# Rows of the first combine loaded ahead of and between the attention's first weight slabs, with the sums of its norm on ScalarE

## The chip, the cores and the metric

The kernel runs on one core of one Trainium2 chip. A core has a matrix engine (TensorE, PE in the profile), a vector engine (VectorE, DVE), an activation engine (ScalarE, ACT), a general engine (GpSimd, POOL) and a queue engine (SyncE, SP) from which nearly all loads are issued. Each engine runs its own instructions in the order in which they stand and waits for the others by semaphores. The metric is the device time of one execution in microseconds; less is better.

## The reference, cut to what matters

Two layers over 1024 tokens of 1024 numbers. Each has a mixer and a mixture of experts (MoE), and each of these four is followed by a layer norm. The change lies where the first layer ends and the second begins:

```
ffn = _hierarchical_moe(x, ...)                          # layer 0
x   = _layer_norm(DEEPNORM_ALPHA * x + ffn, g, b)        # "the first combine"
qkv = x @ w_qkv                                          # layer 1: dilated attention
...
def _layer_norm(x, g, b):
    mu = mean(x);  var = mean((x - mu)**2)
    return (x - mu) * rsqrt(var + 1e-5) * g + b
```

The attention's product needs normed rows, so nothing of it can start before the first tile of 128 rows has its norm.

## The kernel before, in words

Rows are worked on in eight tiles of 128. During the MoE the sum `ALPHA * x + ffn` (divided by `ALPHA`) gathers in a DRAM tensor `S`: GpSimd scatters the experts' outputs into it with an adding DMA (L1111). After the last scatter stands a loop over overflow blocks, which runs zero times on these inputs; all engines meet at its end (L1273).

Then `attn_phase` begins. Its `stream` walks over "pieces" of w_qkv, 512 columns each; piece 0 makes K of the first half. A piece is loaded as four slabs `wr` of 256 rows (L1418); ScalarE rounds each into `wh` (L176), VectorE takes the rest into `wl` (L177). `Moe.rows` loads a tile of `S` into a buffer `pre` (L1297), `Moe.combine` norms it and stores it to the DRAM tensor `x` (L1303). `prep` transposes a normed tile on TensorE (L1454), eight blocks in two halves, into `tr`, and splits each half into `xh` (ScalarE) and `xl` (VectorE). One tile of a piece is then 8 steps of three products, `wh*xh`, `wl*xh`, `wh*xl` (L181 to L183), and its result is taken out as `qk`.

`layer_norm` takes mean and variance on VectorE (two BN_STATS, L190; one BN_AGGR, L192), adds the epsilon (L193), raises to -1/2 on GpSimd (L194), and then makes two passes on VectorE: `(a - mean) * g` (L196) and `a * rstd + b` (L197). The last norm of the kernel, `Moe.finish`, takes its sums on ScalarE instead: a Copy with scale -1/D that accumulates the negative mean (L1316) and a Square that accumulates the variance (L1317).

A scheduler puts the instructions of each engine into one order from the order of the code and its own clock; what it made of the two kernels is shown with the change.

Of the kernel before, what the change touches and what calls it, by code (L numbers as in the profile page):

```python
# [11 lines left out]
F32 = mybir.dt.float32  # L12
# [3 lines left out]
AF = mybir.ActivationFunctionType  # L16
ALU = mybir.AluOpType
# [4 lines left out]
P = 128  # L22
D = 1024
T = 1024
NT = T // P
# [34 lines left out]
BETW = 1  # L60
LATE = (0, 0)
XACT = (0, 1)
EXTRA = 4
HB = 3
CUT = 1
# [14 lines left out]
def dap(ap, off, dims):  # L80
    return bass.AP(tensor=ap.tensor, offset=ap.offset + off, ap=[list(d) for d in dims])
# [104 lines left out]
def layer_norm(nc, cm, pool, dst, src, g, b, last=False, eng=None):  # L186

    st = pool.tile([P, 2, 6], F32, name="ln_st", bufs=2)
    for i in range(2):
        nc.vector.bn_stats(st[:, i, :], src[:, i * 512:(i + 1) * 512])  # L190
    mv = pool.tile([P, 4], F32, name="ln_mv", bufs=2)
    nc.vector.bn_aggr(mv[:, 0:2], st.rearrange("p a b -> p (a b)"))  # L192
    nc.vector.tensor_scalar(mv[:, 2:3], mv[:, 1:2], EPS / ALPHA2, None, op0=ALU.add)  # L193
    nc.gpsimd.tensor_tensor(mv[:, 3:4], mv[:, 2:3], cm.mhalf, op=ALU.pow)  # L194
    if last:
        nc.vector.scalar_tensor_tensor(src, src, mv[:, 0:1], g, op0=ALU.subtract, op1=ALU.mult)  # L196
        nc.vector.scalar_tensor_tensor(dst, src, mv[:, 3:4], b, op0=ALU.mult, op1=ALU.add)  # L197
        return
    nc.vector.scalar_tensor_tensor(mv[:, 2:3], mv[:, 0:1], -1.0, mv[:, 3:4], op0=ALU.mult, op1=ALU.mult)
    nc.scalar.activation(src, src, AF.Identity, scale=mv[:, 3:4], bias=mv[:, 2:3])  # L200
    (eng or nc.vector).tensor_tensor(src, src, g, op=ALU.mult)
    nc.gpsimd.tensor_tensor(dst, src, b, op=ALU.add)
# [735 lines left out]
class Moe:  # L938
# [6 lines left out]
    def run(self, extra=lambda tmp: None):  # L945
# [273 lines left out]
        for n in range(N + 1):  # L1219
            st = steps[n] if n < N else None  # L1220
            before = steps[n - 1] if n else None
            if n == PLAN:
                plan = rt.plan(sp, sp.tile([P, 512], F32, name="h", bufs=2), lambda s: ps.tile(s, F32, name="tr"))
                tab, base = plan[2:]
                more(plan)
            if n == STEPS.index("D") - PLD:
                tok, gate = place(slice(OV, OV + 1), kp.tile([P, 2048], F32, name="pre3"), "tok1")
                d = steps[STEPS.index("D")].blocks[1]
                d.tok, d.gate = tok[:MORE], gate[:MORE]
            if n == 0:  # L1230
                steps[0].x = [rows_in(steps[0], blocks[0])]
            if st:
                gathers(blocks.index(st.blocks[-1]) + 5 if n >= PLAN else FIXED)

            def between():
                if n > 1:
                    rows_out(steps[n - 2])
                if n:
                    before.h = [sides(before, h, "h" + "d" * i) for i, h in enumerate(before.h)]

            if st:
                if n >= FIXED:
                    st.U, st.W = parts(*(of_expert(nc.sync.value_load(tab[0:1, OV + 1 + r:OV + 2 + r], min_val=0, max_val=31))
                                         for r in st.experts))
                if n:
                    load(st.U)
                pg = up(st, between)
            with behind(tc, *first, *self.loads[-1:][:n > 3]):
                if n == 6:
                    t = kp.tile([P, 2048], F32, name="pre4")  # L1250
                    self.lng, self.lnb = t[:, 0:D], t[:, D:]
                    nc.sync.dma_start(self.lng, dap(self.ln_g, 0, [[0, P], [1, D]]))
                    nc.sync.dma_start(self.lnb, dap(self.ln_b, 0, [[0, P], [1, D]]))
                if n == EXTRA:
                    extra(kp.tile([P, D], F32, name="pre2"))
            if n:
                load(before.W)
                if not st:
                    between()
                ws = split_down(before)  # L1260
            if st:
                h = [hidden(b, p, "d" * i) for i, (b, p) in enumerate(zip(st.blocks, pg))]
            if n + 1 < N:
                steps[n + 1].x = [rows_in(steps[n + 1], b, "d" * i) for i, b in enumerate(steps[n + 1].blocks)]
            if n:
                before.p = down(before, ws)
            if st:
                st.h = [hidden_in(x) for x in h]
# [28 lines left out]
        self.tc.nc.sync.dma_start(a, token_rows(self.S, self.rt.runs[i], D))  # L1297
        return a

    def combine(self, i, store):  # L1300
        a = self.rows(i)
        layer_norm(self.tc.nc, self.cm, self.kp, a, a, self.lng, self.lnb, True)
        self.tc.nc.sync.dma_start(token_rows(store, self.rt.runs[i], D), a)  # L1303
        return a

    def finish(self, store):
        nc = self.tc.nc
        rows = [self.rows(i) for i in range(NT)]

        nc.vector.tensor_scalar(self.lng, self.lng, D ** 0.5, None, op0=ALU.mult)  # L1310
        mean, ss = (self.kp.tile([P, NT], F32, name=n) for n in ("f_mean", "f_ss"))
        with self.tc.tile_pool(name="f", bufs=2, reuse_waits="tile") as fp:
            for i in range(NT + 1):
                if i < NT:
                    a, m, s = rows[i], mean[:, i:i + 1], ss[:, i:i + 1]
                    nc.scalar.activation(fp.tile([P, D], F32, name="f_j"), a, AF.Copy, scale=-1 / D, accum_out=m)  # L1316
                    nc.scalar.activation(fp.tile([P, D], F32, name="f_j"), a, AF.Square, bias=m, accum_out=s)  # L1317
                    nc.vector.tensor_scalar(s, s, D * EPS / ALPHA2, None, op0=ALU.add)  # L1318
                    nc.gpsimd.tensor_tensor(s, s, self.cm.mhalf, op=ALU.pow)  # L1319
                    nc.vector.scalar_tensor_tensor(a, a, m, self.lng, op0=ALU.add, op1=ALU.mult)  # L1320
                if i:
                    a, s = rows[i - 1], ss[:, i - 1:i]
                    nc.vector.scalar_tensor_tensor(a, a, s, self.lnb, op0=ALU.mult, op1=ALU.add)  # L1323
                    nc.sync.dma_start(token_rows(store, self.rt.runs[i - 1], D), a)


TWO_PI = 2 * math.pi
# [57 lines left out]
def attn_phase(tc, cm, rope_, xd, before, w_qkv, w_o, ln_g, ln_b, runs, emit):  # L1385
# [6 lines left out]
    with ctx:  # L1392
# [79 lines left out]
        def flip(dst, n, r, tag):  # L1472
# [4 lines left out]
            V.tensor_copy(dst[:, 2 * n:2 * n + a, :], pt)  # L1477
            asked.add(tag)

        def stream():  # L1480

            pieces = [(i, s, 0, 512) for i in range(5) for s in (1, 0, 2)] + [(5, 2, 0, 512)]
# [7 lines left out]
                k -= len(pieces)  # L1490
                return Weights(w_o, 0, 512, slice(k * 512, k * 512 + 512))

            nxt = piece(0).make()
            for c in range(4):
                prep(0, c, before.combine(c, xd))
            pend = []
            for k, (i, s, n, w) in enumerate(pieces):
                g, h = steps[i]
                ws = nxt.make()
                nxt = piece(k + 1).make(1)  # L1500
                if i == 5:
                    yield lambda: 3 in done_att
                for c in range(4):
                    j = 4 * h + c
                    xh, xl = XS[g, j]
                    pq = pmm([P, w])
                    for kk in range(KD):
                        if kk == 4 and w == 512:
                            yield 2700, 0
                        mm3(nc, pq, xh[:, kk, :], xl[:, kk, :], *ws.row(kk), kk == 0, kk == KD - 1)  # L1510
                    if k == 0:
                        before.combine(4 + c, xd)
                        if c == 3:
                            open_late()
                    if s == 2:
                        VT[g, j] = sp.tile([P, 512], F32, name="vt", bufs=8)
                        nc.scalar.activation(VT[g, j], pq, AF.Copy)
                    else:
                        dst = KT if s == 1 else QT
                        if n == 0:  # L1520
                            dst[g, j] = sp.tile([P, 4, P], F32, name="kt" if s == 1 else "qt", bufs=8 if s == 1 else 5)
                        pend.append((dst[g, j], n, rope(g, j, pq), (i, c, n) if s == 0 else None))
                    while len(pend) > (LAG if i < 5 and s != 2 else LAG5 if i == 5 and k + 1 < len(pieces) else 0):
                        flip(*pend.pop(0))
                    if s == 2 and i < 5:
                        g2, h2 = steps[i + 1]
                        for cc in {1: (0,), 2: (1,), 3: (2, 3)}.get(c, ()):
                            prep(g2, 4 * h2 + cc)
                    yield 2700, 0
                if s == 2 and i < 5:  # L1530
                    done_gemm.add(i)
# [291 lines left out]
```

## Time and profile before

| | |
|---|---|
| runs | 2817.41, 2819.85, 2819.84 us; median 2819.84 |
| profiled execution | 2819.68 us, span 2817.9 us |
| busy share | PE 93%, DVE 60%, ACT 44%, POOL 22% |
| mean granted TensorE clock | 0.958 |
| last product of layer 0's MoE | starts at 1463.54 us |
| first transposition of the attention | starts at 1490.76 us |

All places are in us from the start of the span. The hole in TensorE's work between the last two lines is where the change lies; it is about a hundredth of the span.

### The profile page before, as it was taken

Reading aid. Unit: us, or ns where it says so; the run is one execution under the profiler, and the core shown is the slowest. Engines: PE = TensorE matmul, PEld = TensorE weight load, DVE = VectorE, ACT = ScalarE, POOL = GpSimd, SP = SyncE. Lnnn points to the kernel's source line nnn. Section 1 sums busy time; section 2 is a strip of 40 time slices with the busy share of each in tenths; the row PEclk is TensorE's granted clock in tenths of the full one; section 3 lists DMA queues with packets and bytes.
Section 4 is the critical chain, followed back from the end, with each engine's and each line's share of the span. In section 5 each row is a group of like instructions: output and inputs, shape, how many; then the busy total and the mean of one; then the engine's idle time right before and its main releaser. Section 6 shows DMA issues by size and latency. Waiting matters only on the chain. (4 is left out here: it accounts for less than half of the span.)

```text
span 2817.9 us, 40424 instructions
## 1 busy us (share of the span) xinstructions
PE 2609.4 (93%) x14744; PEld 1919.6 (68%) x14744; DVE 1701.0 (60%) x3287; ACT 1250.8 (44%) x1974; POOL 617.5 (22%) x554
## 2 busy tenths in 40 slices
PE   8999999999997999999967999999998899999893
PEld 6778888788874656555636887778886465565562
DVE  5586676897674545645637544555668354466464
ACT  3354443545421544644632444444532254456464
POOL 0054332444351311212111000111112121121112
PEclk9999999999997999999988999999998899999997
DMA  5454543735466899999965432333325899999995
GB/s 147 130 150 135 145 125 105 218 114 155 128 226 223 297 399 378 368 393 373 386 233 213 124 117 73 106 109 107 98 93 195 288 356 387 367 389 388 380 387 190
DMA packets 316415, 647.68 MB, mean 230 GB/s; under 512 B 34172, under 2 KB 202548, under 8 KB 283444
## 3 DMA queue, kind: packets, MB, share of 16 engines
q1 hardware_dynamic: 296660, 594.63, 59.0%
q0 software_dynamic: 14944, 33.64, 5.1%
q10 hardware_dynamic: 4608, 16.78, 1.5%
q8 instruction: 119, 1.95, 0.3%
q14 instruction: 84, 0.69, 0.1%
HBM read 598.15 MB, written 66.19 MB: 236 GB/s over the span
## 5 line engine op out<-in xcount | busy, mean ns | idle before, releaser
L990 DVE TENSOR_TENSOR wl<-wr,wh 128x2048 fp32r<-128x2048 f32 x209 | 477.6, 2291 | 291.9 <-ACT wh L986 227.8
L986 ACT ACTIVATE wh<-wr 128x2048 fp32r<-128x2048 f32 x212 | 405.0, 1916 | 266.0 <-DMA wr<-in_moe_w_down_dram 137.2
L177 DVE TENSOR_TENSOR wl<-wr,wh 128x1024 fp32r<-128x1024 f32 x184 | 239.0, 1300 | 142.2 <-ACT wh L176 137.2
L176 ACT ACTIVATE wh<-wr 128x1024 fp32r<-128x1024 f32 x184 | 194.2, 1055 | 240.5 <-PE mm L182 93.2
L181 PE MATMUL mm<-xth,wh 128*128 128x512 f32 x640 | 255.7, 400 | 1.2 <-DVE carry L391 1.2
L183 PE MATMUL mm<-xth,wl 128*128 128x512 f32 x640 | 254.9, 399 | 0.5 <-DVE wl L177 0.5
L182 PE MATMUL mm<-xtl,wh 128*128 128x512 f32 x640 | 253.3, 396 | 1.7 <-DVE xtl L177 1.7
L181 PE MATMUL mm<-wh,xh 128*128 128x512 f32 (+1 forms) x640 | 248.2, 388 | 0.0
L182 PE MATMUL gu<-wl,xh 128*112 128x512 f32 x576 | 230.3, 400 | 18.2 <-DVE wl L990 15.1
L182 PE MATMUL mm<-wl,xh 128*128 128x512 f32 (+1 forms) x640 | 241.8, 378 | 0.0
L183 PE MATMUL mm<-wh,xl 128*128 128x512 f32 (+1 forms) x640 | 239.8, 375 | 0.0
L181 PE MATMUL gu<-wh,xh 128*112 128x512 f32 x576 | 231.9, 403 | 2.1 <-ACT wh L986 2.0
L183 PE MATMUL gu<-wh,xl 128*112 128x512 f32 x576 | 230.6, 400 | 0.0
L1050 PE MATMUL gu<-wr,xh 128*64 128x512 f32 (+1 forms) x784 | 213.0, 604 | 12.0 <-DMA wr<-in_moe_w_up_dram 11.9
L995 POOL DMA_INDIRECT G<-X,pl_toks x44 | 68.2, 1551 | 557.0 <-PE tr L1011 478.1
L1111 POOL DMA_INDIRECT S<-y,pl_toks x56 | 110.2, 1968 | 327.9 <-ACT y L1109 249.8
L1050 PEld LDWEIGHTS gu<-wr,xh 128*64 128x64 f32 (+1 forms) x784 | 70.3, 145 | 139.3 <-issue 111.3
L182 PEld LDWEIGHTS gu<-wl,xh 128*112 128x112 f32 x576 | 102.0, 177 | 58.3 <-DVE wl L990 21.8
L183 PEld LDWEIGHTS mm<-xth,wl 128*128 128x128 f32 x640 | 121.5, 190 | 27.9 <-issue 1.4
L181 PEld LDWEIGHTS mm<-xth,wh 128*128 128x128 f32 x640 | 121.6, 190 | 27.5 <-issue 1.9
L182 PEld LDWEIGHTS mm<-xtl,wh 128*128 128x128 f32 x640 | 121.4, 190 | 26.7 <-DVE xtl L177 2.0
L182 PE MATMUL dn<-wl,hh 128*112 128x512 f32 x288 | 121.3, 421 | 19.4 <-DVE wl L990 19.4
(485 smaller groups left out, 5404.4 us busy)
## 6 DMA issues: line engine op xcount, KB each, us to landing
wr<-in_moe_w_gate_dram SPq DMA_DIRECT2D x126, 1024.0 KB, 20.4
wr<-in_moe_w_down_dram SPq DMA_DIRECT2D x126, 1024.0 KB, 21.9
wr<-in_moe_w_up_dram SPq DMA_DIRECT2D x124, 1024.0 KB, 21.7
wr<-in_ssd_w_in_dram SPq DMA_DIRECT2D x80, 512.0 KB, 4.0
wr<-in_attn_w_qkv_dram SPq DMA_DIRECT2D x72, 512.0 KB, 4.1
E<-csd SPq DMA_DIRECT2D x32, 512.0 KB, 4.3
wr<-in_ssd_w_out_dram SPq DMA_DIRECT2D x32, 512.0 KB, 4.0
xt<-x SPq DMA_DIRECT2D x24, 512.0 KB, 4.0
```

What stands on the lines that cost most here:

```text
L176: return (nc.scalar.activation(hi, src, AF.Copy), (eng or nc.vector).tensor_tensor(lo, src, hi.bitcast(F32), op=ALU.subtract))
L177: (eng or nc.vector).tensor_tensor(lo, src, hi.bitcast(F32), op=ALU.subtract))
L181: nc.tensor.matmul(out, lhsT=sh, rhs=mh, start=first, stop=False)
L182: nc.tensor.matmul(out, lhsT=sh, rhs=ml, start=False, stop=False)
L183: return nc.tensor.matmul(out, lhsT=sl, rhs=mh, start=False, stop=last)
L986: chain("act", lambda: nc.scalar.activation(wh, wr, AF.Copy))
L990: chain("dve", lambda: nc.vector.tensor_tensor(wl, wr, wh.bitcast(F32), op=ALU.subtract), *gate)
L995: return nc.gpsimd.indirect_dma_start(out=g[:r], out_offset=None, in_=rt.X[:, :], in_offset=bass.IndirectOffsetOnAxis(ap=tok, axis=0), bou ...
L1050: i = nc.tensor.matmul(out[c], lhsT=x[k][:, c], rhs=w[z][:, n], start=first, stop=last)
L1111: nc.gpsimd.indirect_dma_start(out=S[:, :], out_offset=bass.IndirectOffsetOnAxis(ap=tok, axis=0), in_=y[:tok.shape[0]], in_offset=None, bo ...
```

## The change

Four things. (1) `Moe.combine` falls into three: `rows` (the load), `norm` and `normed`. The attention now issues the load of row tile 0 first, then one weight slab of piece 0 and one row tile in turn, and the loads of tiles 5 to 7 after them. Before, all four slabs stood first. (2) The norm is that of `finish`: sums by ScalarE for tiles 1 to 7. Tile 0 keeps BN_STATS, with two small instructions in place of one. The junk output of the two ScalarE passes goes to the buffers `xt`, which the attention uses later. (3) The scaling of `g` by the square root of D, which the form with sums needs, moves from `finish` into the MoE (step 16 in the code) and is done in both layers. (4) `finish` calls the same functions and is otherwise as it was.

```diff
+SCALE = 16
...
+                if n == SCALE:
+                    nc.vector.tensor_scalar(self.lng, self.lng, D ** 0.5, None, op0=ALU.mult)
...
-    def combine(self, i, store):
-        a = self.rows(i)
-        layer_norm(self.tc.nc, self.cm, self.kp, a, a, self.lng, self.lnb, True)
-        self.tc.nc.sync.dma_start(token_rows(store, self.rt.runs[i], D), a)
-        return a
+    def norm(self, i, a, junk, last=False):
...
+        if i or last:
+            nc.scalar.activation(junk(), a, AF.Copy, scale=-1 / D, accum_out=m)
+            nc.scalar.activation(junk(), a, AF.Square, bias=m, accum_out=s)
+            nc.vector.tensor_scalar(s, s, D * EPS / ALPHA2, None, op0=ALU.add)
+        else:
...
+            nc.vector.tensor_scalar(s, mv[:, 1:2], float(D), D * EPS / ALPHA2, op0=ALU.mult, op1=ALU.add)
+            nc.vector.tensor_scalar(m, mv[:, 0:1], -1.0, None, op0=ALU.mult)
+        nc.gpsimd.tensor_tensor(s, s, self.cm.mhalf, op=ALU.pow)
+        nc.vector.scalar_tensor_tensor(a, a, m, self.lng, op0=ALU.add, op1=ALU.mult)
...
+    def normed(self, i, a, store):
+        self.tc.nc.vector.scalar_tensor_tensor(a, a, self.ss[:, i:i + 1], self.lnb, op0=ALU.mult, op1=ALU.add)
         self.tc.nc.sync.dma_start(token_rows(store, self.rt.runs[i], D), a)
...
-            nxt = piece(0).make()
+            nxt, rows = piece(0), [before.rows(0)]
             for c in range(4):
-                prep(0, c, before.combine(c, xd))
+                nxt.make(c + 1)
+                rows.append(before.rows(c + 1))
+                combine(c, rows[c])
+                prep(0, c, rows[c])
+            rows += [before.rows(c) for c in range(5, 8)]
...
                     if k == 0:
-                        before.combine(4 + c, xd)
+                        combine(4 + c, rows[4 + c])
```

SP's queue right behind the loop, before. `pre_13170` holds row tiles 0 and 1, `pre_13225` tiles 2 and 3, and so on; `S_237` is `S`, `x_83` is `x`.

```order
L1418 DMA wr<-in_attn_w_qkv_dram 128x2x512 x4
L1297 DMA pre_13170<-S_237 128x1024 x2
L1297 DMA pre_13225<-S_237 128x1024 x2
L1297 DMA pre_13311<-S_237 128x1024 x2
L1297 DMA pre_13408<-S_237 128x1024
L1418 DMA wr<-in_attn_w_qkv_dram 128x2x512
L1297 DMA pre_13408<-S_237 128x1024
L1418 DMA wr<-in_attn_w_qkv_dram 128x2x512 x3
L1303 DMA x_83<-pre_13170 128x1024 x2
```

The same place of the change (`pre_13147` holds row tiles 0 and 1, `pre_13191` tiles 2 and 3).

```order
L1300 DMA pre_13147<-S_237 128x1024
L1431 DMA wr<-in_attn_w_qkv_dram 128x2x512
L1300 DMA pre_13147<-S_237 128x1024
L1431 DMA wr<-in_attn_w_qkv_dram 128x2x512
L1300 DMA pre_13191<-S_237 128x1024
...
L1300 DMA pre_13284<-S_237 128x1024 x2
L1431 DMA wr<-in_attn_w_qkv_dram 128x2x512
L1328 DMA x_83<-pre_13147 128x1024
L1431 DMA wr<-in_attn_w_qkv_dram 128x2x512
L1328 DMA x_83<-pre_13147 128x1024
```

Row tile 0 went from the fifth place to the first. The three further slabs of piece 1, which stood ahead of all stores of normed rows, now stand one behind each of the first stores.

VectorE's queue at the same place, before.

```order
L177 TENSOR_TENSOR wl<-wr,wh 128x1024 x4
L190 BN_STATS ln_st<-pre_13170 128x6 x4
L192 BN_AGGR ln_mv<-ln_st 128x2 x2
L193 TENSOR_SCALAR ln_mv<-ln_mv 128x1
L196 SCALAR_TENSOR_TENSOR pre_13170<-pre_13170,ln_mv,pre_9802 128x1024
L190 BN_STATS ln_st<-pre_13225 128x6
...
L197 SCALAR_TENSOR_TENSOR pre_13170<-pre_13170,ln_mv,pre_9802 128x1024 x2
...
L177 TENSOR_TENSOR xl<-tr,xh 128x512 x2
```

And in the change (`pre_9802` is the tile with `g` and `b`).

```order
L1317 BN_STATS ln_st<-pre_13147 128x6 x2
L1319 BN_AGGR ln_mv<-ln_st 128x2
L1320 TENSOR_SCALAR f_ss<-ln_mv 128x1
L1321 TENSOR_SCALAR f_mean<-ln_mv 128x1
L1323 SCALAR_TENSOR_TENSOR pre_13147<-pre_13147,f_mean,pre_9802 128x1024
L178 TENSOR_TENSOR wl<-wr,wh 128x1024
L1327 SCALAR_TENSOR_TENSOR pre_13147<-pre_13147,f_ss,pre_9802 128x1024
L1313 TENSOR_SCALAR f_ss<-f_ss 128x1
L1323 SCALAR_TENSOR_TENSOR pre_13147<-pre_13147,f_mean,pre_9802 128x1024
L178 TENSOR_TENSOR wl<-wr,wh 128x1024
L1327 SCALAR_TENSOR_TENSOR pre_13147<-pre_13147,f_ss,pre_9802 128x1024
L178 TENSOR_TENSOR xl<-tr,xh 128x512
```

Before, four slab splits and the statistics of two tiles stood ahead of tile 0's norm, and the first `xl` stood behind both passes of tiles 0 and 1, the first passes of tiles 2 and 3 and the statistics of further tiles. Now tile 0's norm has one split in it, and the first `xl` stands behind the norm of tile 1.

## Rows read from the trace of the kernel before

**Rows 1.** Windows: us, busy us of PE, PEld, DVE, ACT, POOL; clock; DMA share; GB/s.

```profile
1475.00:1490.00 15.00, 0.00 (x0) 0.00 (x0) 12.89 (x19) 4.59 (x5) 3.07 (x2) 0.50 1.04 414
1500.00:1510.00 10.00, 10.00 (x39) 7.97 (x39) 10.00 (x16) 2.25 (x4) 2.71 (x2) 0.77 0.31 127
...
1600.00:1700.00 100.00, 100.00 (x771) 80.42 (x771) 49.45 (x164) 44.92 (x104) 0.00 (x0) 1.00 0.35 107
...
2000.00:2100.00 100.00, 100.00 (x783) 87.09 (x779) 64.45 (x257) 44.17 (x131) 16.83 (x14) 1.00 0.25 80
```

**Rows 2.** Waits, 1455 to 1540: us in total, times, longest.

```profile
PE tr L1454 <- DVE pre L197: 26.8, 1, 26.8
...
PE tr L1454 <- DVE xl L177: 5.0, 1, 5.0
```

**Rows 3.** Timeline of SP's queue: start, us from first to last, line, issues.

```profile
1471.73 1.93 SPq L1418 DMA_DIRECT2D wr<-in_attn_w_qkv_dram  x4
1473.70 4.96 SPq L1297 DMA_DIRECT2D pre<-S  x7
...
1482.19 2.81 SPq L1418 DMA_DIRECT2D wr<-in_attn_w_qkv_dram  x3
```

**Rows 4.** Timeline of ScalarE: the first two slabs and the fourth tile's eviction.

```profile
1475.65 1.06 ACT L176 ACTIVATE wh<-wr 128x1024 fp32r<-128x1024 f32 x1 [11.09 <-DMA wr<-in_attn_w_qkv_dram]
...
1477.00 1.06 ACT L176 ACTIVATE wh<-wr 128x1024 fp32r<-128x1024 f32 x1 [0.29 <-DMA wr<-in_attn_w_qkv_dram]
...
1527.01 0.60 ACT L1461 ACTIVATE qk<-mm 128x512 f32<-128x512 f32 x1 [0.37 <-PE mm L183]
```

**Rows 5.** Timeline of VectorE, 1455 to 1500.

```profile
1476.74 5.27 DVE L177 TENSOR_TENSOR wl<-wr,wh 128x1024 fp32r<-128x1024 f32 x4 [17.42 <-ACT wh L176]
1481.93 2.46 DVE L190 BATCH_NORM_STATS2 ln_st<-pre 128x6 f32<-128x512 f32 x4
1484.31 0.33 DVE L192 BATCH_NORM_AGGREGATE ln_mv<-ln_st 128x2 f32<-128x12 f32 x2
...
1484.61 1.28 DVE L196 SCALAR_TENSOR_TENSOR pre<-pre,ln_mv,pre 128x1024 f32<-128x1024 f32 x1
1485.80 0.68 DVE L190 BATCH_NORM_STATS2 ln_st<-pre 128x6 f32<-128x512 f32 x1
...
1498.09 1.27 DVE L177 TENSOR_TENSOR xl<-tr,xh 128x512 fp32r<-128x512 f32 x2
```

**Rows 6.** Timeline of TensorE at the end of its two waits.

```profile
1490.76 1.97 PE L1454 MATMUL tr<-ident,pre 128*128 128x128 f32 x8 [26.83 <-DVE pre L197]
...
1498.82 1.11 PE L1454 MATMUL tr<-ident,pre 128*128 128x128 f32 x4 [5.04 <-DVE xl L177]
```

**Rows 7.** Timeline of SP's queue at the kernel's end.

```profile
2786.09 3.94 SPq L1297 DMA_DIRECT2D pre<-S  x8
```

**Rows 8.** Timeline of ScalarE at the kernel's end.

```profile
2789.94 1.06 ACT L1316 ACTIVATE f_j<-pre 128x1024 f32<-128x1024 f32 x1 [11.79 <-DMA pre<-S]
...
2792.27 1.04 ACT L1316 ACTIVATE f_j<-pre 128x1024 f32<-128x1024 f32 x1
```

**Rows 9.** All eight raisings to -1/2 of the first combine, grouped by line.

```profile
L194 POOL TENSOR_TENSOR ln_mv<-ln_mv,mhalf 128x1 f32<-128x1 f32 x8 | 13.0, 1632 | 37.5 <-DVE ln_mv L193 37.5
```

**Rows 10.** Window of TensorE alone in which its clock rose: busy, clock, DMA, GB/s.

```profile
1504.00:1505.00 1.00, 1.00 (x6) 0.68 0.00 0
```

**Rows 11.** Waits of SP's queue, 2060 to 2770.

```profile
SPq L971 <- DMA S<-xt: 53.2, 1, 53.2
```

**Rows 12.** Windows in layer 1's MoE, columns as in rows 1.

```profile
2400.00:2500.00 100.00, 96.99 (x438) 60.79 (x437) 53.80 (x37) 52.18 (x49) 18.83 (x11) 0.97 0.99 370
```

**Rows 13.** The scaling of g before (layer 1), by its line.

```profile
L1310 DVE TENSOR_SCALAR pre<-pre x1: 687/687/687, 2327.1 to 2327.1; 128x1024 f32<-128x1024 f32 x1
```

**Rows 14.** Timeline of VectorE in layer 0's MoE, near the new scaling's place.

```profile
1006.41 4.50 DVE L990 TENSOR_TENSOR wl<-wr,wh 128x2048 fp32r<-128x2048 f32 x2 [0.39 <-ACT wh L986]
1014.37 2.29 DVE L990 TENSOR_TENSOR wl<-wr,wh 128x2048 fp32r<-128x2048 f32 x1 [3.46 <-PE gu L183]
```

More of the change, by code (lines that the diff above doesn't have):

```diff
@@ L1298, in rows @@
         return a
-    def combine(self, i, store):
-        a = self.rows(i)
-        layer_norm(self.tc.nc, self.cm, self.kp, a, a, self.lng, self.lnb, True)
+    def norm(self, i, a, junk, last=False):
+        nc = self.tc.nc
+        if not i:
+            self.mean, self.ss = (self.kp.tile([P, NT], F32, name=n) for n in ("f_mean", "f_ss"))
+        m, s = self.mean[:, i:i + 1], self.ss[:, i:i + 1]
+        if i or last:
[3 more added lines that the diff above has]
+        else:
+            st = self.kp.tile([P, 2, 6], F32, name="ln_st", bufs=2)
+            for k in range(2):
+                nc.vector.bn_stats(st[:, k, :], a[:, k * 512:(k + 1) * 512])
+            mv = self.kp.tile([P, 4], F32, name="ln_mv", bufs=2)
+            nc.vector.bn_aggr(mv[:, 0:2], st.rearrange("p a b -> p (a b)"))
+            nc.vector.tensor_scalar(s, mv[:, 1:2], float(D), D * EPS / ALPHA2, op0=ALU.mult, op1=ALU.add)
[4 more added lines that the diff above has]
+        self.tc.nc.vector.scalar_tensor_tensor(a, a, self.ss[:, i:i + 1], self.lnb, op0=ALU.mult, op1=ALU.add)
         self.tc.nc.sync.dma_start(token_rows(store, self.rt.runs[i], D), a)
-        return a
     def finish(self, store):
-        nc = self.tc.nc
         rows = [self.rows(i) for i in range(NT)]
-        nc.vector.tensor_scalar(self.lng, self.lng, D ** 0.5, None, op0=ALU.mult)
-        mean, ss = (self.kp.tile([P, NT], F32, name=n) for n in ("f_mean", "f_ss"))
         with self.tc.tile_pool(name="f", bufs=2, reuse_waits="tile") as fp:
@@ L1314, in finish @@
                 if i < NT:
[L1315 to L1320, printed above, removed]
+                    self.norm(i, rows[i], lambda: fp.tile([P, D], F32, name="f_j"), True)
                 if i:
-                    a, s = rows[i - 1], ss[:, i - 1:i]
-                    nc.vector.scalar_tensor_tensor(a, a, s, self.lnb, op0=ALU.mult, op1=ALU.add)
-                    nc.sync.dma_start(token_rows(store, self.rt.runs[i - 1], D), a)
+                    self.normed(i - 1, rows[i - 1], store)
 TWO_PI = 2 * math.pi
@@ L1478, in flip, with combine @@
             asked.add(tag)
+        def combine(i, a):
+            before.norm(i, a, lambda: sp.tile([P, D], F32, name="xt", bufs=4))
+            before.normed(i, a, xd)
         def stream():
```

## The prediction

> **What bounds the kernel now.** I read the windows first, then the waits, then the queues one by one around the place that the windows point to. In the window from 1475 to 1490 TensorE does nothing at all, while VectorE is busy for 12.89 of 15 us; from 1500 on TensorE is busy for the whole of every window shown, and it stays so through the attention (five windows of 100 us between 1600 and 2100, the first and the last in [rows 1]). So the stretch after the loop is bound by VectorE, and all that follows up to about 2100 by TensorE: what lets TensorE start earlier there moves the whole attention. The waits say the same: the first transposition waits 26.8 us for the second pass of the norm, and after three us of work TensorE waits another 5.0 us for the first `xl` [rows 2]. The queues say why. SP issues four slabs from 1471.73, and the rows of `S` only from 1473.70 [rows 3]; the slabs land 1.35 us apart (1475.65, 1477.00, [rows 4]), and VectorE, which keeps its order, splits all four (5.27 us) before it looks at a row, so its first statistics start at 1481.93 [rows 5]. TensorE starts at 1490.76, and works without a gap from 1498.82 [rows 6].
>
> **The change part by part.** The sum is the move of that 1498.82, built up along VectorE's new order.
>
> *Rows first.* Tile 0's load is now the first issue behind the loop, at 1471.73. How soon such a load lands when it stands first is shown at the kernel's end: issued at 2786.09, used at 2789.94, so 3.85 us [rows 7, 8]. Tile 0 is there at 1475.6. Slabs and rows are both 512 KB; at 1.35 us apiece slab 0 lands at 1476.9, tile 1 at 1478.3, slab 1 at 1479.6.
>
> *Tile 0's norm.* Two BN_STATS take half of the 2.46 us of four, 1.23, to 1476.8. The aggregation and two small instructions take what two aggregations and one small one took, 1484.31 to 1484.61, so 0.3, to 1477.1. A pass over a tile keeps VectorE for 1.20 us (1484.61 to 1485.80), to 1478.3. Then stands slab 0's split, a quarter of 5.27 us, so 1.32; its `wh` is ready at 1476.9 + 1.06 = 1478.0, in time; to 1479.6. The raising on GpSimd (mean 1.63, [rows 9]) began at 1477.1 and ends under these two. Second pass, to 1480.8 [all durations from rows 5]. The first transposition can start there, 9.9 us sooner than 1490.76.
>
> *Tile 1's sums on ScalarE.* Copy and Square of one tile take 2792.27 - 2789.94 = 2.33 us [rows 8]. From 1478.3 they end at 1480.6, before VectorE is free: this is work taken off VectorE (1.23 + 0.2 us a tile, seven times) and put on an engine that is busy 4.59 of 15 and 2.25 of 10 us there [rows 1]. ScalarE's added 7 x 2.33 = 16.3 us lie beside VectorE's work as long as no Square ends after VectorE asks for it; I cost them at nothing for tile 1, and take the rest up as a rival.
>
> *The first xl.* From 1480.9: pass 1 of tile 1 to 1482.1, slab 1's split (`wh` at 1480.6 + 1.06 = 1481.7) to 1483.4, pass 2 to 1484.6, `xl` (half of 1.27) to 1485.2. Before, TensorE worked on behind that `xl` from 1498.82. The difference is 13.6 us.
>
> *From there to the end of piece 0.* Before, the four tiles took until 1527.0, when the fourth is taken out [rows 4]: 28.2 us, of which TensorE ran the first 5.8 at half rate, since its clock rises between 1504 and 1505 (mean 0.68 in that window, [rows 10]). With the same 28.2 the new end is 1513.4. The other limit is VectorE. Its work from 1475.6 to the last `xl` of piece 0 is 1.5 (tile 0's statistics) + 16 passes x 1.20 + 5 splits x 1.32 + 8 `xl` x 0.63 + about 2 of small ones and of the rotation of two results, so 34 us, to 1509.8. Half a tile of products follows; 28.2 us with 5.8 at half rate are 25.3 at full rate for four tiles, so half a tile is 3.2, to 1513.0. TensorE's limit is the later by a little, so 13.6 us stand, and more than 14 cannot come out here.
>
> *SP's stores between the slabs of piece 1.* Their loads now stand behind stores that wait for normed tiles (1480.8, 1484.6, and, with the same steps carried on for tiles 2 and 3, 1489.5 and 1495.1). The last slab of piece 1 is so issued by about 1495 and lands by 1499, where it was issued by 1485 [rows 3]. Piece 1 begins at 1513; the cover is 14 us, and this costs nothing. If it were gone, each us of lateness would be one on the path.
>
> *Scaling g in the MoE.* One instruction of 0.69 us [rows 13]. In layer 1 it was already there, since the scheduler had pulled it out of `finish`. In layer 0 it is new and stands between the two splits that start at 1006.41; VectorE waits 3.46 us soon after [rows 14]. I take nothing, and 0.7 as the upper bound.
>
> The sum: 2819.68 - 13.6 = 2806.1 us for the profiled execution, which lies 0.16 under the median of the runs; I say 2806.
>
> **A rule weighed.** TensorE stood still for 26.8 us [rows 2], its clock went to half rate (0.50 in the first window of [rows 1]), and it rose only 5.8 us after the work had become gapless; the three us of work from 1490.76 that a wait ended did not lift it [rows 6, 10]. The Trainium skill ("TensorE: Matmul & The Clock Gate", section "HAM oscillation — how this bites in real kernels") says that the throttled rate is the default and that matmul work in bursts with waits between them keeps falling back to it. By that rule an earlier start with small waits in it gains less than the start moves. The trace agrees so far as it goes. The row alone gives -13.6, the rule the time of the first rival.
>
> **The rivals.**
>
> *The clock stays at half rate through the new stretch.* In the new order TensorE is fed in portions: `xl` of tile 2 stands on VectorE behind two passes and a split, at about 1500 to 1501. If the small waits before it keep the clock at 1.2 GHz until then, instead of 1491, ten us are worked at half rate and five are lost: -8.6, 2811. For it: the burst of [rows 6] that did not lift the clock. Against: behind 1485.2 my steps leave no wait over 1 us.
>
> *ScalarE's sums arrive late.* ScalarE keeps its order, and its Copies wait for rows to land ahead of `xh` evictions that TensorE needs. Sums 16.3, five slabs 5.2, eight `xh` and two `qk` 5.6 us: 27 us in the same 34. Each Square that ends after VectorE asks for it adds to VectorE's limit. Two or three late by 1.5 to 2 us cost 4: 2810. For it: slack of only a few us on either engine. Against: tile 1's sum, the tightest, is in time by 0.3.
>
> *The gain is given back later.* Layer 1's MoE keeps the DMA engines at a share of 0.99 [rows 12]. Were its weight stream to start no sooner, the time would stay 2819.7. Against: the first wait of that stream on SP's queue is one of 53.2 us for a result of the attention [rows 11], which comes sooner with it.
>
> *Slower: SP's queue holds the weights back.* SP issues nothing while it waits for a store. If a normed tile comes late, all slabs behind it are late; piece 1's last slab, wanted some 4 us into the piece, must be issued by about 1513 (3.85 us to land). From there each us costs one; at 1527 the gain is gone, and at 1530 the time is 2823. That needs tile 3's norm to end 35 us behind my 1495, 9 us more for each of the first four. For it: the order on SP. Against: nothing in the trace makes a tile's norm that long.
>
> **How the numbers follow.** Forecast, 2804 to 2808: 0.60. Clock low: 0.12. Late sums: 0.16. Given back: 0.07. Slower: 0.05. The two middle rivals give 2810 to 2812, so the range ends at 2812; below, VectorE's limit (-14) and the runs' own spread of 2.4 us give 2803. A measurement can tell about 0.2%, 5.6 us, from no change, so faster means under 2814.2: 0.60 + 0.12 + 0.16 = 0.88; same 0.08 (given back, with the milder half of slower); slower 0.04.
>
> **What would show it.** In the new profile the first transposition starts near 1481 and the first `wh*xl` product near 1485; the fourth `qk` of piece 0 is taken out near 1513; the windows through the attention stay full; the end of the attention and the span move by the same amount. A first transposition at 1481 with a fourth `qk` later than 1516 makes the feeding steps wrong (the clock row tells which rival); a moved `qk` without a moved span makes the third rival right.

## The result, and the profile after

The change takes 2803.48 us (median of 6 runs, 2799.09 to 2807.32) where the kernel before took 2819.07 beside it (6 runs, 2817.41 to 2823.37): a ratio of 0.9945, 95% interval 0.9935 to 0.9956. That is 15.6 us, by the interval 12 to 18. The profiled execution took 2806.40 us (before 2819.68), so 13.3 less; the forecast was 2806.1. Two executions, one of e3_warm (2979.07 us, mean granted clock 0.817) and one of the change beside e9_filled_again (4532.87 us, 0.715), ran at a lower clock and are left out of every time and comparison here.

Two executions start the stretch of the change at slightly different places (the last product of layer 0's MoE at 1463.54 before, at 1462.56 after). So from here on a place is also given in us behind that product, which is called P. From P to the end of the span it is 1354.4 us before and 1342.1 after: of the 13.3 us, 12.3 lie behind P and 1.0 ahead of it.

The first windows, to be laid beside [rows 1] (columns as there):

```profile
1475.00:1490.00 15.00, 8.64 (x25) 6.57 (x26) 14.45 (x20) 13.96 (x22) 4.75 (x3) 0.50 1.03 399
1490.00:1500.00 10.00, 10.00 (x50) 8.18 (x50) 10.00 (x16) 10.00 (x20) 5.90 (x3) 0.99 1.04 407
1600.00:1700.00 100.00, 100.00 (x764) 80.53 (x762) 48.01 (x160) 46.21 (x108) 0.00 (x0) 1.00 0.33 103
```

TensorE is busy for 8.64 us of a window in which it did nothing, and for all of the next. The price stands in ScalarE's column: from 1475 to 1500 it is busy for 23.96 of 25 us. The attention further on is as it was.

The waits from 1465 to 1540 that answer to [rows 2] (us in total, times, longest):

```profile
PE tr L1467 <- DVE pre L1327: 16.9, 1, 16.9
...
PE tr L1467 <- DVE f_ss L1313: 1.3, 1, 1.3
DVE pre L1327 <- POOL f_ss L1322: 0.5, 1, 0.5
ACT xt L1311 <- DMA pre<-S: 0.2, 1, 0.2
PE mm L182 <- ACT xh L177: 0.2, 1, 0.2
```

26.8 became 16.9, and 5.0 became 1.3. The last three are what the prediction costed at nothing, and together they are under 1 us. The 1.3 is written down to the small instruction behind the first `xl`; what TensorE waited for is that `xl`.

VectorE's new order, for [rows 5]:

```profile
1474.34 1.29 DVE L1317 BATCH_NORM_STATS2 ln_st<-pre 128x6 f32<-128x512 f32 x2 [16.15 <-DMA pre<-S]
...
1478.49 1.28 DVE L1327 SCALAR_TENSOR_TENSOR pre<-pre,f_ss,pre 128x1024 f32<-128x1024 f32 x1
1479.68 0.15 DVE L1313 TENSOR_SCALAR f_ss<-f_ss 128x1 f32<-128x1 f32 x1
...
1482.61 1.28 DVE L1327 SCALAR_TENSOR_TENSOR pre<-pre,f_ss,pre 128x1024 f32<-128x1024 f32 x1 [0.45 <-POOL f_ss L1322]
1483.81 0.68 DVE L178 TENSOR_TENSOR xl<-tr,xh 128x512 fp32r<-128x512 f32 x1
...
1507.26 0.68 DVE L178 TENSOR_TENSOR xl<-tr,xh 128x512 fp32r<-128x512 f32 x1
```

SP had issued tile 0's load at 1470.80; VectorE starts on it 3.54 us later (the forecast took 3.85). The first `xl` ends at 1484.49, and the last of piece 0 at 1507.94. ScalarE, GpSimd and TensorE beside it:

```profile
1478.21 1.15 ACT L1312 ACTIVATE xt<-pre,f_mean 128x1024 f32<-128x1024 f32 x1
1479.27 0.19 ACT L1312 ACTIVATION_READ_ACCUMULATOR xt<-pre,f_mean 128x1 f32 x1
...
1479.92 2.66 POOL L1322 TENSOR_TENSOR f_ss<-f_ss,mhalf 128x1 f32<-128x1 f32 x1 [3.20 <-DVE f_ss L1313]
```

```profile
1479.82 1.97 PE L1467 MATMUL tr<-ident,pre 128*128 128x128 f32 x8 [16.87 <-DVE pre L1327]
...
1484.55 1.12 PE L1467 MATMUL tr<-ident,pre 128*128 128x128 f32 x4 [1.35 <-DVE f_ss L1313]
1485.31 0.78 PE L184 MATMUL mm<-wh,xl 128*128 128x512 f32 x1
...
1489.73 0.63 PE L182 MATMUL mm<-wh,xh 128*128 128x512 f32 x1
1490.15 0.44 PE L183 MATMUL mm<-wl,xh 128*128 128x512 f32 x1
```

Tile 1's sum is there at 1479.46, and VectorE asks for it at 1479.68. The raising of that sum takes GpSimd 2.66 us, and VectorE waits 0.45 us for it. Behind the first `xl` TensorE works without a gap; its products take 0.63 us each until the clock rises at about 1490.2 (0.50 before, 0.99 behind, in the windows above).

In the later rows little else changed. The long wait of layer 1's weight stream is 53.5 us, was 53.2 [rows 11], and the first load behind it is issued at 2111.48 where it was issued at 2125.52, so the stream moved with the attention. The scaling of `g` shows up twice, 0.69 us each, at 1007.8 and 2312.7:

```profile
SPq L972 <- DMA S<-xt: 53.5, 1, 53.5
```

```profile
L1256 DVE TENSOR_SCALAR pre<-pre x2: 687/688/689, 1007.8 to 2312.7; 128x1024 f32<-128x1024 f32 x2
```

### The profile page after: what moved, and what is told of

Its sections match the earlier page's. It is cut to its first block, busy times and chain, and to the rows that moved or that the text cites. A ratio compares the mean times of both kernels' runs of the same rounds, so it can differ in the third digit from the quotient of the medians.

```text
span 2804.7 us, 40430 instructions
## 1 busy us (share of the span) xinstructions
PE 2606.4 (93%) x14744; PEld 1918.7 (68%) x14744; DVE 1690.6 (60%) x3268; ACT 1266.0 (45%) x2002; POOL 618.3 (22%) x554
## 5 line engine op out<-in xcount | busy, mean ns | idle before, releaser
L182 PEld LDWEIGHTS mm<-xth,wh 128*128 128x128 f32 x640 | 121.6, 190 | 28.2 <-issue 1.9
```

Of the source, the lines that this page charges most:

```text
L182: nc.tensor.matmul(out, lhsT=sh, rhs=mh, start=first, stop=False)
```

## The experiments

All places in this table are us behind P, read from the timelines. "First transposition" and "resumes" are the starts of TensorE's `tr` and of its first `wh*xl`; "piece 0" is the end of the last product of piece 0's fourth tile; "last vt" is the start of the last `vt` eviction, near the end of the attention's products; "last y" that of the last expert output of layer 1.

| kernel | first transposition | resumes | piece 0 | last vt | last y |
|---|---|---|---|---|---|
| before | 27.22 | 36.04 | 63.38 | 542.31 | 1314.01 |
| the change | 17.26 | 22.75 | 49.49 | 528.94 | 1301.09 |
| e7_after_again | 17.47 | 22.97 | 49.48 | 528.94 | 1300.55 |
| e9_after_beside | 16.84 | 22.33 | 48.55 | 528.00 | 1298.78 |
| e1_loads_only | 18.03 | 23.47 | 58.26 | 537.20 | 1307.25 |
| e2_sums_only | 23.71 | 29.98 | 57.16 | 536.13 | 1307.90 |
| e4_more_act | 17.07 | 23.17 | 50.07 | 529.03 | 1300.29 |
| e5_all_sums | 17.97 | 23.47 | 49.83 | 529.28 | 1300.98 |
| e3b_warm | 16.83 | 22.11 | 49.02 | 528.46 | 1300.32 |
| e6_warm_pool | 16.99 | 22.39 | 50.63 | 530.07 | 1301.57 |
| e8_warm_filled | 17.31 | 21.91 | 47.27 | 526.46 | 1297.47 |
| e9_filled_again | 16.62 | 21.94 | 47.28 | 526.51 | 1298.70 |

The column "piece 0" does not hold the same work in all rows. A finished tile's `qk` is later transposed on TensorE in a group of four blocks. Two such groups stand ahead of the end of piece 0 in the kernel before (where that end is at 1526.92):

```profile
1520.80 0.60 PE L1476 MATMUL tr<-ident,qk 128*128 128x128 f32 x4
...
1524.01 0.60 PE L1476 MATMUL tr<-ident,qk 128*128 128x128 f32 x4
```

In the change the scheduler put the second one behind it (the end is at 1512.05):

```profile
1506.42 0.60 PE L1489 MATMUL tr<-ident,qk 128*128 128x128 f32 x4
...
1513.48 0.60 PE L1489 MATMUL tr<-ident,qk 128*128 128x128 f32 x4
```

e1, e2 and e4 have two groups in piece 0 like the kernel before, all other rows have one like the change. A group is worth 0.5 us: from piece 0's end to piece 1's it is 23.7 us with four groups and 24.2 with five. So rows with a different number of groups are compared at the last `vt`.

**One part alone.** e1_loads_only keeps the new order of loads and takes the statistics of all tiles on VectorE:

```diff
-        if i or last:
+        if last:
```

> The new load order with BN_STATS for all eight tiles (no sums on ScalarE in the first combine). All anchors are taken from the last product of layer 0's MoE, as differences to the kernel before. Theory: the load order moves the first transposition (about -9), but VectorE keeps 7 x 1.4 = 10 us more work than in the change, and piece 0 becomes VectorE's: end of piece 0 at -4 to -7, time 2813 to 2816. Rival (the load order is the whole gain, the sums on ScalarE only move work off an engine that did not limit): end of piece 0 at -13, time 2805 to 2807.

e2_sums_only keeps ScalarE's sums and puts the loads back into the old order:

```diff
-            nxt, rows = piece(0), [before.rows(0)]
+            nxt, rows = piece(0).make(), []
...
-                nxt.make(c + 1)
-                rows.append(before.rows(c + 1))
+                rows.append(before.rows(c))
...
-            rows += [before.rows(c) for c in range(5, 8)]
...
+                        rows.append(before.rows(4 + c))
```

> The old load order (four slabs first) with the sums of tiles 1 to 7 on ScalarE. Theory: four splits still stand ahead of tile 0's norm; first transposition -3 to -4, first xl about -6, end of piece 0 -6, time about 2813. Rival (the load order is the whole gain): within 2 us of before, 2817 to 2820.

Times: e1 2810.56 us (ratio to before 0.998, 0.9969 to 0.9991), e2 2809.72 (0.9972, 0.9961 to 0.9982). Both times lie below what was expected (2813 to 2816, and about 2813), while the ends of piece 0 are as expected: 5.1 and 6.2 us sooner than before. At the last `vt` it is the same 5.1 and 6.2; together 11.3, where the change has 13.4. Both rivals, by which the load order is the whole gain, are refuted. Each part alone meets the limit that the other removes. e1 has its first transposition 9.2 us sooner, almost as the change, and then TensorE waits for VectorE (waits, 1455 to 1540):

```profile
PE tr L1467 <- DVE pre L1327: 17.6, 1, 17.6
PE tr L1467 <- DVE xl L178: 5.0, 1, 5.0
PE mm L184 <- DVE xl L178: 1.8, 1, 1.8
```

and in that 5.0 us its clock falls, so that the products at 1500 run at 0.63 us each once more:

```profile
1493.81 0.40 PE L183 MATMUL mm<-wl,xh 128*128 128x512 f32 x1
1499.20 1.11 PE L1467 MATMUL tr<-ident,pre 128*128 128x128 f32 x4 [5.00 <-DVE xl L178]
1499.97 0.78 PE L184 MATMUL mm<-wh,xl 128*128 128x512 f32 x1
1500.54 0.63 PE L182 MATMUL mm<-wh,xh 128*128 128x512 f32 x1
```

e2 still has the four splits ahead of its first statistics, as [rows 5] have, and its first transposition is only 3.5 us sooner:

```profile
1473.50 5.28 DVE L178 TENSOR_TENSOR wl<-wr,wh 128x1024 fp32r<-128x1024 f32 x4 [17.29 <-DMA wr<-in_attn_w_qkv_dram]
1478.70 1.28 DVE L1317 BATCH_NORM_STATS2 ln_st<-pre 128x6 f32<-128x512 f32 x2
```

**Is ScalarE near its limit?** e4_more_act makes the Copy pass twice for tiles 1 to 7:

```diff
+            if not last:
+                nc.scalar.activation(junk(), a, AF.Copy, scale=-1 / D, accum_out=m)
             nc.scalar.activation(junk(), a, AF.Copy, scale=-1 / D, accum_out=m)
```

> The change, with the Copy pass of tiles 1 to 7 done twice: about 1.1 us more on ScalarE per tile, 7.7 in all, same result. Theory (ScalarE's sums lie beside VectorE's work with little slack: 13.96 of 15 us busy, tile 1's Square ends 0.2 us before VectorE asks): first xl +1 to +2, end of piece 0 +2 to +5 against the change. Rival (ScalarE has room): within 1 us of the change.

2805.49 us (0.9964, 0.995 to 0.9978), and piece 0 ends 0.6 us later than in the change, of which 0.5 is the group of transpositions; at the last `vt` 0.1 is left. Seven passes of 1.06 us and their reads of the accumulator (0.19 us) are 8.8 us more work on an engine that was busy for 24 of 25 us, and almost nothing came of it: ScalarE's work spreads into the ten us from 37.4 behind P on, where it is busy for 9.13 us instead of 3.86 (the change first, e4 second; columns as in [rows 1]):

```profile
1500.00:1510.00 10.00, 10.00 (x51) 8.32 (x50) 9.65 (x17) 3.86 (x6) 3.24 (x2) 1.00 0.81 262
```

```profile
1496.36:1506.36 10.00, 10.00 (x53) 8.23 (x52) 8.45 (x16) 9.13 (x17) 3.04 (x2) 1.00 0.45 164
```

VectorE waits 1.5 us for one sum (`DVE f_ss` on `ACT xt`), and TensorE for nothing over 1.2 us behind the first transposition. ScalarE's window in the change was full because it ran ahead: the sums of tiles 2 to 7 were there 1.2 to 3.3 us before VectorE asked for them.

e5_all_sums takes tile 0's sums on ScalarE too (`if i or last:` becomes `if True:`).

> The change with the sums of tile 0 on ScalarE as well. Tile 0 is ready for its first pass 2.33 us after landing instead of 1.8, and the first slab and tile 1 wait behind its sums on ScalarE: first transposition +0.5, first xl +0.5 to +1 against the change. VectorE has 1.5 us less to do, so the end of piece 0 lies between -0.5 and +1. Rival (ScalarE's order does not matter here): every anchor within 0.3 us.

2806.64 us (0.9964, 0.9948 to 0.9981). The first transposition is 0.7 us later than in the change (0.5 later than in the latest of its three traces) and piece 0 ends 0.3 later: Copy and Square take 2.43 us where two BN_STATS and the aggregation take 1.5. So the exception for tile 0 brings the first transposition forward; the 0.3 at the end of piece 0 is less than the change's own traces differ by (48.55 to 49.49), and what the exception is worth there is not shown.

**Does the half rate cost anything?** e3_warm and e3b_warm are the same kernel: the change with 40 transpositions of the identity, unused, ahead of the first row.

```diff
             nxt, rows = piece(0), [before.rows(0)]
+            for _ in range(10):
+                pt = pmm([P, 4, P], "tr", 2)
+                for k in range(4):
+                    nc.tensor.transpose(pt[:, k, :], cm.ident, cm.ident)
```

> The change, with 40 transpositions of the identity (their result is not used) put on TensorE between the loop and the first row, so that its clock does not stand at half rate when the rows come. Theory (TensorE's and VectorE's limits lie within 1 us of each other at the end of piece 0): the first products run at full rate, but piece 0 ends at most 1 us sooner than in the change, time 0 to 1 us less. Rival (half rate alone sets the end of piece 0): 2.9 us sooner, half of the 5.8 us at half rate.

e3_warm took 2804.10 us (0.995, 0.9934 to 0.9967). Its trace is not used here; e3b_warm is the same kernel again, for another trace.

> The kernel of the run before with 40 transpositions of the identity ahead of the first row, once more, for a trace at the full clock. Theory: piece 0 ends at most 1 us sooner than in the change (VectorE's last xl holds it). Rival (half rate alone sets the end of piece 0): 2.9 us sooner. Both times lie within 3 us of the change.

2804.63 us (0.996, 0.9943 to 0.9976). The transpositions raised the clock, and it fell again before the products came (windows of e3b):

```profile
1478.00:1480.00 2.00, 0.73 (x2) 0.30 (x2) 2.00 (x2) 2.00 (x5) 0.35 (x1) 1.00 1.05 407
1480.00:1482.00 2.00, 1.08 (x5) 1.08 (x6) 2.00 (x5) 2.00 (x4) 0.40 (x1) 0.53 1.05 418
1482.00:1486.00 4.00, 4.00 (x11) 3.13 (x10) 3.56 (x4) 4.00 (x7) 2.26 (x1) 0.50 1.00 358
```

TensorE had three waits there, of 1.3, 1.6 and 1.1 us; the clock fell 0.3 us into the third, at about 1480.1. So the products ran at half rate as before, and the run says nothing on what that costs.

e6_warm_pool adds to it that GpSimd splits the third and the fourth slab of piece 0, to take load off VectorE.

```diff
-            split(nc, wh, wl, wr)
+            made.append(1)
+            split(nc, wh, wl, wr, nc.gpsimd if len(made) in (3, 4) else None)
...
```

> The change with the 40 transpositions and with the rest wl of the third and fourth slab of piece 0 made on GpSimd (about 2.4 us each) instead of VectorE: both limits are loosened at once. Theory (two limits within 1 us of each other): piece 0 ends 1.5 to 2.9 us sooner than in the change, more than with the transpositions alone, and the time is 1 to 3 us less. Rival (one limit only): the same as with the transpositions alone.

2808.3 us (0.9962, 0.9949 to 0.9976); piece 0 ends 1.1 us later than in the change, so the gain did not come. But the run loosened neither limit and decides nothing between the two: the clock fell here too (0.50 from 1484 to 1490), and the splits came late. A split takes GpSimd 2.4 us against VectorE's 1.22, a raising stands between the two and others behind them, and TensorE waits for `xl` three times, 3.4 us in total:

```profile
1486.56 2.38 POOL L178 TENSOR_TENSOR wl<-wr,wh 128x1024 fp32r<-128x1024 f32 x1 [2.02 <-ACT wh L177]
1488.90 1.53 POOL L1322 TENSOR_TENSOR f_ss<-f_ss,mhalf 128x1 f32<-128x1 f32 x1
1490.40 2.41 POOL L178 TENSOR_TENSOR wl<-wr,wh 128x1024 fp32r<-128x1024 f32 x1
```

e7_after_again is the change once more, for the scatter of these places.

> The change itself, unchanged, beside the other three on the same chip: -13 to -16 us against before, and every anchor of its first trace within 0.5 us as counted from the last product of layer 0's MoE.

2803.51 us (0.9954, 0.9942 to 0.9966); all places to piece 0 and the last `vt` agree within 0.25 us with the first trace. The last `y` lies 0.54 sooner, just outside the 0.5 that was expected.

e8_warm_filled keeps the clock up: beside the 40 transpositions it has 24 unused ones of tile 0's normed row, and they fill the two waits behind the first transpositions.

```diff
...
+            keep_busy(40, cm.ident)
...
                 prep(0, c, rows[c])
+                if not c:
+                    keep_busy(24, rows[0][:, 0:P])
```

> The change, with TensorE kept busy: 40 transpositions of the identity into an unused buffer ahead of the first row's (as in e3b), and 24 unused ones of tile 0's normed row in the places where TensorE waited 1.3 and 2.8 us in the change's trace, so that the clock is still at full rate when the first products of piece 0 start. Theory (two limits near each other): the half-rate products, which last until 27 us behind the last product of layer 0's MoE in the change, go, worth some 2.9 us to TensorE, but the last xl of piece 0 stays at 45.3 us behind that product and about 3.2 us of products follow it; so piece 0 ends 0 to 1.5 us sooner than in the change (48.0 to 49.5), and behind the last of these TensorE shows waits for VectorE's xl. Rival (half rate alone sets the end): 2.9 us sooner, 46.6, about 2800.5. If the granted clock falls all the same before the first products, the run tells nothing of the two.

2803.13 us (0.9949, 0.9933 to 0.9966), which can't be told from the change's. The clock holds at 1.00:

```profile
1480.00:1482.00 2.00, 2.00 (x12) 1.70 (x11) 2.00 (x4) 2.00 (x4) 1.59 (x1) 1.00 1.03 412
...
1486.00:1488.00 2.00, 2.00 (x13) 1.64 (x12) 2.00 (x6) 2.00 (x5) 1.52 (x1) 1.00 1.05 415
```

Piece 0 ends at 47.27, 2.2 us sooner than in the change's first two traces: more than the two-limits theory gave (0 to 1.5), less than half rate alone (2.9). Not all of it comes from the products: TensorE resumes 0.8 us sooner, 0.4 of it because the four transpositions ahead run at full rate, the rest because the first `xl` is done 0.5 sooner, as it is in one of the change's own traces (e9_after_beside). From there to the end it takes 25.4 us against 26.7. The two-limits theory took the last `xl` of piece 0 to stay at 45.3; it ended at 44.2, because the scheduler put one of the 16 passes of the norm behind it:

```profile
1501.76 0.70 DVE L178 TENSOR_TENSOR xl<-tr,xh 128x512 fp32r<-128x512 f32 x1
...
1503.15 1.29 DVE L1327 SCALAR_TENSOR_TENSOR pre<-pre,f_ss,pre 128x1024 f32<-128x1024 f32 x1
```

From that `xl` to the end are 3.0 us, in the change 4.1. The first product that reads it starts 0.8 us after it here and 2.1 in the change, so the last `xl` held the end in neither. The waits for `xl` that it expected behind the half-rate products do not show: behind the resumption TensorE waits only 0.4 us, for a slab's `wl`. So TensorE's own work set the end of piece 0 in the change.

**A version that may beat both.** e8's kernel and the change side by side on one chip:

> The kernel of e8_warm_filled once more, beside the change on the same chip, as a version that may beat both kernels. By e8's trace (clock held; piece 0 ends 47.3 us behind the last product of layer 0's MoE, 2.2 sooner than in the change, and the end of layer 1's attention is 2.5 sooner) it should be 2 to 3 us faster than the change, about 0.1%, with piece 0's end again at 47.0 to 47.6. If e8's gain was chance of one execution, piece 0 ends at 48.5 or later and the two times agree within 1 us.

> The change, as the partner of e9_filled_again in the same job. Piece 0 ends 49.5 us (+-0.3) behind the last product of layer 0's MoE, as in its two traces so far; the time is 2803 to 2806.

2802.01 us (0.9944, 0.9931 to 0.9957) against 2803.21 (0.9946, 0.9933 to 0.9959): the order expected, but a difference that these times can't tell from none. The places can, as far as the attention goes: piece 0 ends at 47.28 again, and the last `vt` is 1.5 us ahead of the partner's. At the last `y` only 0.1 us of that is left, so it is not shown that this version is faster as a whole. The change missed its own expectation; piece 0 ended at 48.55, not at 49.5. TensorE resumed 0.42 us sooner than in its first trace, and the clock rose sooner. Its products at half rate are those from the first to the second of these rows, 7 in all, where the first trace has 11 and starts a twelfth:

```profile
1486.42 0.78 PE L184 MATMUL mm<-wh,xl 128*128 128x512 f32 x1
...
1489.13 0.57 PE L184 MATMUL mm<-wh,xl 128*128 128x512 f32 x1
1489.54 0.39 PE L182 MATMUL mm<-wh,xh 128*128 128x512 f32 x1
```

Products follow one another 0.43 us apart at half rate and 0.23 at full, and over these products the lead grows from 0.42 to 1.29 us: 0.87 us from the clock, without any added instruction. At the end of piece 0 0.94 is left. The rest is lost at the fourth tile's first transpositions, which now come before VectorE has read the buffer `tr` that they write:

```profile
1500.54 0.42 PEld L1467 LDWEIGHTS tr<-ident,pre 128*128 128x128 f32 x4 [0.54 <-DVE xl L178]
```

So half-rate products do delay the end of piece 0, and the two limits do lie near each other in the change's order: with TensorE 1.3 us ahead, VectorE begins to hold it.

## Why the prediction was right

- *What bounds.* Right: TensorE started sooner, and the attention moved as a whole. Behind P the gain is 13.4 us at the last `vt`, 12.9 at the last `y` and 12.3 at the end of the span. The given-back rival (2819.7) is refuted by these rows. That the profiled time shows 13.3, so near the forecast 13.6, is in part luck: 1.0 of it lies ahead of P, and no run ties that to the change.
- *Rows first, tile 0's norm.* The first transposition is 9.96 us sooner behind P (forecast 9.9).
- *Sums on ScalarE.* Tile 1's are 0.2 us early (forecast 0.3). The late-sums rival is wrong, and by more than the prediction thought: e4 loads ScalarE with 8.8 us more, for 0.1 at the last `vt`. The prediction read "slack of only a few us" from two sums of busy time; it did not ask by when each piece of work was due.
- *The first xl.* TensorE resumes 13.3 us sooner (forecast 13.6). The load landed 0.3 us sooner than forecast. Against that stands VectorE's wait of 0.45 us for tile 1's raising, which has no term in the sum; it took 2.66 us, and the prediction had taken the mean of 1.63 for tile 0's [rows 9].
- *To the end of piece 0.* 26.7 us from there; by the same places 27.3 in the trace of before, with one group of transpositions more. The prediction's 28.2 runs to the eviction of the fourth `qk`. That came at 1514.42 (forecast 1513.4), 11.6 us sooner behind P, since ScalarE took it out 2.4 us after the last product (0.1 before); TensorE waited for nothing there. TensorE's limit was the later one, as forecast, but with more room: the last `xl` was done 2.1 us before a product read it, where the prediction had the two limits 0.4 apart. VectorE's sum was right (33.6 us from the first statistics to the last `xl`, forecast 34); the half tile of 3.2 us behind that `xl` was too long, for only 2.0 us of products had to wait for it. And "more than 14 cannot come out here" was wrong: e8 has 16.1, and the change itself 14.8 in e9_after_beside (14.3 at the last `vt`). The sum took all 16 passes to stand ahead of the last `xl`, which is an order and not a limit.
- *The clock.* The rival that it stays at half rate until 1500 is wrong: it rose at 1490.2, 5.7 us after the gapless work began (1484.55), as before (5.8); in e9_after_beside it took 3.8. The Trainium skill ("TensorE: Matmul & The Clock Gate", section "HAM oscillation — how this bites in real kernels") has matmul bursts with waits between them falling back to the low rate. e1 (0.63 us products behind its wait of 5.0) and e3b (with waits of 1.1 to 1.6) agree with it. In the change the work behind the first `xl` has no such wait. From there to the end of piece 0 the half rate costs about 1.4 us (26.7 against 25.4 in e8, with the order a little different).
- *SP's stores, scaling of g.* The stores cost nothing, as forecast: in piece 1 TensorE waits for no slab, and the last of them is issued at 1489.84 (forecast by about 1495). The distance from piece 0's to piece 1's end is 24.2 us, 23.7 before; that 0.5 us is the group of transpositions that moved, and no loss. The scaling of `g` stands ahead of P. All that shows of it is that TensorE waits 1.3 us for the next split (at 1016) where it waited 1.0, and P itself is no later.
- *The median.* 2.3 us more than the profiled difference came out between the medians, and the median of 2803.48 lies 0.5 us below the forecast's band (2804 to 2808), 0.5 above the lower end of the range. P lies 1.0 us sooner in the trace after, and in the change's three traces it lay between 1458.7 and 1464.1. That scatter, ahead of the change's place, is larger than the 2.3; no run here was made to explain it, so the cause of the 2.3 is open.

## What to carry to other kernels

When a hole has a chain through several engines, walk the queues in order and add up durations: both the move of the first transposition and of the resumption came out within 0.3 us in the first trace and within 0.6 in the other two. Two repairs of one hole need not add up; each may hide the limit that the other takes away, so one alone looks like half a success (5.1 and 6.2 against 13.4). And an engine that is busy all through a window is not a bound by that: ask when the work was due before calling it full. Before two kernels are compared at a place, see that the same work stands ahead of it: a group of transpositions that the scheduler moved was 0.5 us here.

## What the runs showed that was not expected

- The clock, once up, was lost although no wait was longer than 1.6 us (e3b; it fell in the third of three), and held when unused transpositions filled the last two of them, though the first, now of 1.6 us, was still there (e8).
- The same kernel's clock rose behind 11 products at half rate in one execution and behind 7 in another; that alone was 0.9 us.
